# Down phase of a ConvFFN: four inner activations loaded earlier, a store moved to another queue

## The chip, the cores and the metric

The kernel runs on one core of a Trainium2 chip. The metric is the device time of one execution in microseconds. Its engines: PE (TensorE, matmuls), DVE (VectorE), ACT (ScalarE), POOL (GpSimd), and SP (SyncE), whose queue starts nearly all DMA transfers. Each engine works through its own instructions in order. Line numbers (L1347) are those of the kernel before.

## The reference, cut to what matters

Two layers work on 128 context rows and 1024 latent rows (1152 rows, 9 tiles of 128). The change lies in the ConvFFN that ends both layers:

```python
def _conv_ffn(h, w_up, conv_w, w_down):          # h: 1152 x 1024, w_up: 1024 x 5632, w_down: 2816 x 1024
    u = _dwconv(h @ w_up, conv_w)                # three taps along the rows
    a, gt = jnp.split(u, 2, axis=-1)
    return (jax.nn.silu(gt) * a) @ w_down
...
    xs = _layer_norm(ALPHA * xs + gt2_s * fs, ln2_g[l], ln2_b[l])
```

## The kernel before, in words

All matmuls are single precision made of three products of a high and a low part (`mm3`, L93 to L95): `hi` is a rounded copy made by ACT, `lo` the rest, made by DVE or POOL. For weights that is `wsplit` (L108, L109), for inner activations `split_s` (L1267, L1268).

The instructions stand in each engine's queue in the order in which the Python code issues them; no scheduler moves them. A pool gives tiles of one tag a ring of buffers; a pool that is closed gives its memory to the pools opened after it, and the first writer of new memory waits for the last readers of the tile that lay there.

**Up phase** (`ffn_up`). The 22 inner features blocks of 128 are made as pairs: block f of `a` with block f of the gate. The first three pairs are plain products, pairs p = 3 to 21 use seven products q = 0 to 6 on quarter matrices, whose weight operands are sums held in the tag `S`. The results of a pair gather in a tile `u` (two buffers, taken in turn). A pair's convolution, silu and product t1*t2 run on ACT and DVE while the next pair's products run on PE; `keep` (L1130) then stores it to DRAM as sd[l][p], from SP. The last pair (p = 21) has no next pair: its convolution runs after the last product. In its course the first two weight units of the down phase (`raws`, split into `dws`) and the activations f = 0, 1 (`sraws`, L1196) are loaded, and f = 0, 1 are split.

**Down phase** (`ffn_down`). The blocks f are taken in groups: [0, 1], then five of four. Within a group, for each half of the 1024 output columns, nine row tiles t = 8 to 0 are multiplied: 6 matmuls a tile in the first group, 12 later. A tile goes to one of six PSUM banks (`psd`). In the first group ACT copies it to y[t] (L1347), later DVE adds it (L1349). Between the tiles, weight units are split and loaded (`split_unit`, `raw_unit`) and the activations of the next group are split. `split_s` takes the oldest loaded activation and then loads the one two further into the same buffer (`sraw`, L1254). In the first group f = 2 to 5 are split behind the tiles t = 7, 5, 4, 2 of the first half. The residual stream of the groups after it uses `gb` (L298), two rows of layer-norm gains spread to all partitions, scaled on ACT behind the first tile of the second group.

SP's order at the seam: weight units 0 and 1, f = 0, 1, the store of pair 20, the store of pair 21, weight units 2 and 3, f = 2, 3, `gb`, then what the splits release.

Of the kernel before, what the change touches and what calls it, by code (L numbers as in the profile page):

```python
# [9 lines left out]
F32 = mybir.dt.float32  # L10
# [10 lines left out]
P = 128  # L21
D = 1024
KT = 8
NT = 9
# [14 lines left out]
HW = 580  # L39
HO = HW - 2  # L40
# [6 lines left out]
FGROUPS = [[0, 1], [2, 3, 4, 5], [6, 7, 8, 9], [10, 11, 12, 13], [14, 15, 16, 17], [18, 19, 20, 21]]  # L47
# [33 lines left out]
def build(tc, ins, outs, consts):  # L81
    nc = tc.nc
# [20 lines left out]
    def wsplit(raw, a, b, ring=None, eng=None):  # L103
        n = a * b
        pool, bufs = ring or (wp, 3)
        hi = pool.tile([P, 1024], F32R, tag="whi", bufs=bufs, name="whi")
        lo = pool.tile([P, 1024], F32R, tag="wlo", bufs=bufs, name="wlo")
        nc.scalar.activation(hi[:, :n], raw[:, :n], AF.Copy)  # L108
        (eng or nc.gpsimd).tensor_tensor(lo[:, :n], raw[:, :n], r32(hi[:, :n]), op=ALU.subtract)  # L109
        return (hi[:, :n].rearrange("p (a b) -> p a b", b=b),  # L110
                lo[:, :n].rearrange("p (a b) -> p a b", b=b))
# [535 lines left out]
    with ExitStack() as st:  # L647
# [185 lines left out]
        with tc.manual_schedule(engines={ET.PE, ET.Activation}):  # L833
# [3 lines left out]
            for i in range(-LEAD - 3, total + PVL):  # L837
                p = i + LEAD
# [143 lines left out]
    sraws = []  # L982
    def ffn_up(l, hT, mod_list, steps, y):
# [9 lines left out]
        ws = {0: wpre.pop(0), 1: wpre.pop(0)}  # L993
        raws = {2: wraw(*up_cols(l, 2))}
        pss, cvs = {}, {}

        def bank():
            return pd.tile([P, 512], F32, tag="d", name="psl")
# [38 lines left out]
        tp, ts, held = None, {}, None  # L1037
# [89 lines left out]
                                               op1=ALU.add)  # L1127

        def keep(p, t):
            nc.sync.dma_start(sd[l][p][:, :2 * HO].rearrange("p (a b) -> p a b", b=HO), t)  # L1130

        for n in range(N0):
            if n == 0:
# [47 lines left out]
        for p in range(P0, NP):  # L1181
            last = p == NP - 1
            u = tp.tile([P, 4, HW], F32, tag="u", bufs=2, name="u")
            us = [u[:, 2 * x:2 * x + 2, :] for x in range(2)]
            e1 = fp.tile([P, HW], F32, tag="e1", name="e1")
            for q in range(7):
                o = 7 * (p - P0) + q
                operand(o + 4)
                if last and q == 2:
                    for x in range(2):  # L1190
                        raws[x] = wraw(*down_unit(l, x))
                if last and q == 2:
                    for f in range(2):
                        raw = tp.tile([P, 4, HW], F32, tag=f"T2{f}", name="sraw").rearrange(
                            "p a b -> p (a b)")[:, :2 * HO]
                        nc.sync.dma_start(raw, sd[l][f][:, :2 * HO])  # L1196
                        sraws.append(raw)
                if last and q == 4:
                    dws[0] = wsplit(*raws.pop(0))
                if last and q > 4:  # L1200
                    split_s(l, q - 5, None)
                ps = pq.tile([P, 2, 512], F32, tag="q", name="psq")

                if old and q == 0:
                    old["t2"] = conv_first(p - 1, 1, old["us"][1])
                    conv_rest(p - 1, 1, old["us"][1], old["t2"])
                    old["t1"] = conv_first(p - 1, 0, old["us"][0])
                if old and q == 1:
                    nc.scalar.activation(old["t2"], old["t2"], AF.Silu)
                    conv_rest(p - 1, 0, old["us"][0], old["t1"])  # L1210
                if old and q == 2:
                    nc.vector.tensor_tensor(old["t1"], old["t1"], old["t2"], op=ALU.mult)
                if old and q == 3:
                    keep(p - 1, old["t1"])
                    if p == P0 + 12:
                        gate_store(l, 5)
                product(o, ps)
                add = nc.vector.tensor_tensor
                b, e = ps[:, :, :HW // 2], two(e1)
                c11, c12, c21, c22 = (two(u[:, x, :]) for x in range(4))  # L1220
                if q == 0:
                    nc.scalar.activation(e, b, AF.Copy)
                elif q == 1:
                    add(c12, e, b, op=ALU.add)
                elif q == 2:
                    add(c21, c12, b, op=ALU.add)
                elif q == 3:
                    add(c22, c21, b, op=ALU.add)
                    add(c12, c12, b, op=ALU.add)
                elif q == 4:  # L1230
                    add(c11, e, b, op=ALU.add)
                elif q == 5:
                    add(c21, c21, b, op=ALU.add)
                elif q == 6:
                    add(c12, c12, b, op=ALU.add)
                if o % 4 == 1 and p < NP - 1:
                    next(mod, None)
            old = {"us": us}
# [5 lines left out]
        conv_rest(NP - 1, 0, us[0], t1)  # L1244
        dws[1] = wsplit(*raws.pop(1))
        nc.vector.tensor_tensor(t1, t1, t2, op=ALU.mult)
        keep(NP - 1, t1)
        tps.close()
        fs.close()
# [2 lines left out]
    def sraw(l, f, pool):  # L1252
        raw = pool.tile([P, 2 * HO], F32, tag="sraw", bufs=2, name="sraw")
        nc.sync.dma_start(raw, sd[l][f][:, :2 * HO])  # L1254
        return raw
# [16 lines left out]
    def ffn_down(l, xsrc, mod_list, dw, tail, pre):  # L1272
        with ExitStack() as st:
# [31 lines left out]
            def x1_pair(n):  # L1305

                if n < 18:
                    xx = x1_tile()
                    for a in range(2):
                        hf, t = (n + a) // 9, NT - 1 - (n + a) % 9  # L1310
                        xxs[n + a] = xx[:, a * 512:(a + 1) * 512]
                        nc.sync.dma_start(xxs[n + a], rows_of(xsum, t)[:, hf * 512:(hf + 1) * 512])
            nf = 2
            raw_unit(2)
            raw_unit(3)
            while len(sraws) < 2:
                sraws.append(sraw(l, 2 + len(sraws), dw))

            gb = affine_rows(lp, l, 0)
            xsum = xh[1]  # L1320

            def residual_of(t, gb):
# [7 lines left out]
                yield  # L1330
                nc.sync.dma_start(rows_of(xsum, t), x)
                yield
            stream = [s for t in range(NT - 1, -1, -1) for s in (residual_of(t, gb),) * 6]
            mod = mod_steps(mod_list, lp, lbank, 1, 3)
            for gi, grp in enumerate(FGROUPS[:-1]):
                for hf in range(2):
                    cols = slice(hf * 512, (hf + 1) * 512)
                    units = [hf] if gi == 0 else [4 * gi - 2 + 2 * hf, 4 * gi - 1 + 2 * hf]
                    nxt = [2, 3] if units == [1] else [] if gi == 0 else [units[0] + 2, units[0] + 3]
                    last = gi == len(FGROUPS) - 2  # L1340
                    if last and hf:
                        nxt += [units[0] + 4]
                    for t in range(NT - 1, -1, -1):
                        ps = pd.tile([P, 512], F32, tag="d", name="psd")
                        products(ps, gi, t, units)
                        if gi == 0:
                            nc.scalar.activation(y[t][:, cols], ps, AF.Copy)  # L1347
                        else:
                            nc.vector.tensor_tensor(y[t][:, cols], y[t][:, cols], ps, op=ALU.add)  # L1349
                        if t in (8, 6, 3) and nxt:  # L1350
                            u = nxt.pop(0)
                            split_unit(u)
                            raw_unit(u + 2)
                        if t in (7, 5, 4, 2) and nf < FGROUPS[gi + 1][-1] + 1 and (t > 3 or gi == 0):
                            if gi == 0 or nf < FGROUPS[gi + 1][0] + 2 * (hf + 1):
                                split_s(l, nf, dw)
                                nf += 1
                        if gi == 1 and t == 1 and hf == 0:
                            gate_load(l, 5, rows)
                        if gi == len(FGROUPS) - 3 and t == 1 and hf:  # L1360
                            x1_pair(0)
                        if gi == 1 and hf == 0 and t == NT - 1:
                            nc.scalar.activation(gb, gb, AF.Copy, scale=ALPHA)
                        if gi and stream:
                            next(stream.pop(0))
                        if gi:
                            next(mod, None)
                        if last and l and t == 8 and hf == 0:
                            gb = affine_rows(lp, l, 1)
                        if last:  # L1370

                            yy = y[t][:, cols]
                            n = 9 * hf + NT - 1 - t
                            if n % 2 == 0:
                                x1_pair(n + 2)
                            nc.gpsimd.tensor_tensor(yy, yy, rows[:, cond_of(t), cols], op=ALU.mult)
                            later.append((yy, xxs.pop(n)))
                            if len(later) > 2:
                                a, b = later.pop(0)
                                nc.vector.tensor_tensor(a, a, b, op=ALU.add)  # L1380
# [733 lines left out]
```

## Time and profile before

| | us |
|---|---|
| median of three runs | 3277.81 |
| lowest, highest | 3276.28, 3280.92 |
| profiled execution, its own time | 3279.65 |
| its span, first to last instruction | 3277.9 |

PE is busy 3144.1 us (96%), DVE 2248.1 (69%), POOL 1421.4 (43%), ACT 1289.4 (39%). The granted TensorE clock is 0.986 of full speed on average. The first down group lies at 1218 to 1254 us in layer 0 and at 2971 to 3007 us in layer 1. In a timeline row the two numbers are start and length in us, then engine, line, operation, out<-in, the count of merged instructions, and in brackets how long the engine had idled and for whom.

### The profile page before, as it was taken

What the parts mean: (1) busy time and instruction counts of PE and PEld (TensorE: products, weight loads), DVE (VectorE), ACT (ScalarE), POOL (GpSimd) and SP (SyncE); (2) the same over time, 40 slices, a digit from 0 to 9 for tenths busy, and PEclk for the clock granted to TensorE, in tenths of its full rate; (3) what the DMA queues carried; (4) which work ended last, traced back from release to release, by engine and by line L of the source; (5) the groups of instructions that cost most, each with busy time, mean ns of one, the idle gap of its engine ahead of it and who ended that gap; (6) DMA issues with size and microseconds to landing.
All of it is one profiled execution on the core that took longest, in us unless ns stands there. A gap on an engine that the chain in (4) does not pass through costs nothing. (4 is left out here: it accounts for less than half of the span.)

```text
span 3277.9 us, 48732 instructions
## 1 busy us (share of the span) xinstructions
PE 3144.1 (96%) x19231; PEld 2910.5 (89%) x19231; DVE 2248.1 (69%) x3117; ACT 1289.4 (39%) x2162; POOL 1421.4 (43%) x1007
## 2 busy tenths in 40 slices
PE   7989999899999998998999999999999999998997
PEld 6989888789999997877999999999779999997886
DVE  6778888548988875674466666655556888774356
ACT  4311998333333333115433334343444333334112
POOL 6821332335545534562244343333425554443565
PEclk9999999999999999999999999999999999999999
DMA  7152000322322326541222222211331323225452
GB/s 220 35 136 90 1 1 8 129 84 68 96 92 86 89 82 210 175 153 64 95 85 75 64 68 81 59 56 37 117 116 53 100 77 97 74 68 181 150 170 84
DMA packets 267476, 305.42 MB, mean 93 GB/s; under 512 B 19587, under 2 KB 200015, under 8 KB 267248
## 3 DMA queue, kind: packets, MB, share of 16 engines
q1 hardware_dynamic: 266448, 300.67, 29.0%
q8 instruction: 152, 2.49, 0.3%
q0 software_dynamic: 800, 1.63, 0.2%
q14 instruction: 76, 0.62, 0.1%
HBM read 237.84 MB, written 64.42 MB: 92 GB/s over the span
## 5 line engine op out<-in xcount | busy, mean ns | idle before, releaser
L1098 POOL TENSOR_TENSOR wlo<-S,whi 128x512 fp32r<-128x512 f32 x152 | 245.0, 1626 | 250.8 <-ACT whi L1097 249.5
L93 PE MATMUL psd<-whi,s 128*128 128x512 f32 x720 | 286.1, 397 | 18.0 <-ACT y L1347 17.0
L109 POOL TENSOR_TENSOR wlo<-wraw,whi 128x1024 fp32r<-128x1024 f32 x78 | 196.3, 2520 | 232.5 <-ACT whi L108 221.7
L94 PE MATMUL psd<-wlo,s 128*128 128x512 f32 x720 | 285.1, 396 | 0.0
L95 PE MATMUL psd<-whi,s 128*128 128x512 f32 x720 | 285.0, 396 | 0.0
L1630 POOL TENSOR_TENSOR X<-X,tot 128x384 f32<-128x384 f32 x144 | 181.0, 1257 | 228.4 <-PE pss L1624 175.6
L1126 DVE SCALAR_TENSOR_TENSOR t<-u,fcw,t 128x1156 f32<-128x1156 f32 x152 | 262.8, 1747 | 13.5 <-ACT t L1121 10.8
L95 PE MATMUL psq<-T,wlo 128*128 128x290 f32 x912 | 270.8, 297 | 0.0
L94 PE MATMUL psq<-T,whi 128*128 128x290 f32 x912 | 270.3, 296 | 0.0
L93 PE MATMUL psq<-T,whi 128*128 128x290 f32 x912 | 270.1, 296 | 0.0
L1098 POOL TENSOR_TENSOR wlo<-wraw,whi 128x512 fp32r<-128x512 f32 x114 | 182.6, 1603 | 172.3 <-ACT whi L1097 156.6
L108 ACT ACTIVATE whi<-wraw 128x1024 fp32r<-128x1024 f32 x130 | 136.7, 1054 | 289.8 <-DMA wraw<-in_ffn_w_down_dram 120.9
L1097 ACT ACTIVATE whi<-S 128x512 fp32r<-128x512 f32 x152 | 92.9, 628 | 323.1 <-DVE S L1076 247.3
L1349 DVE TENSOR_TENSOR y<-y,psd 128x512 f32<-128x512 f32 x144 | 98.0, 684 | 170.9 <-PE psd L95 170.4
L213 DVE SCALAR_TENSOR_TENSOR macc<-mraw,sil,macc 128x512 f32<-128x512 f32 x182 | 192.1, 1095 | 7.3 <-DMA mraw<-in_w_mod_dram 7.3
L93 PE MATMUL psu<-h,whi 128*128 128x388 f32 (+1 forms) x504 | 175.0, 348 | 12.7 <-DVE sc L639 7.3
L93 PEld LDWEIGHTS psd<-whi,s 128*128 128x128 f32 x720 | 136.1, 189 | 52.3 <-ACT y L1347 19.5
L1630 DVE TENSOR_TENSOR X<-X,tot 128x384 f32<-128x384 f32 x144 | 102.5, 712 | 114.1 <-PE pss L1624 76.5
L1624 PE MATMUL pss<-X,km 128*128 128x128 f32 x1008 | 153.0, 289 | 24.3 <-POOL X L1630 10.4
L94 PE MATMUL psu<-h,whi 128*128 128x388 f32 (+1 forms) x504 | 174.4, 346 | 1.9 <-POOL h L428 1.9
L93 PE MATMUL psp<-s,whi 128*128 128x384 f32 x480 | 174.8, 364 | 0.0
L95 PE MATMUL psu<-h,wlo 128*128 128x388 f32 (+1 forms) x504 | 173.2, 344 | 0.0
(438 smaller groups left out, 10046.7 us busy)
## 6 DMA issues: line engine op xcount, KB each, us to landing
wraw<-in_ffn_w_up_dram SPq DMA_DIRECT2D x88, 512.0 KB, 3.8
mraw<-in_w_mod_dram SPq DMA_DIRECT2D x104, 256.0 KB, 2.8
sraw<-sd SPq DMA_DIRECT2D x44, 578.0 KB, 4.6
wraw<-in_ffn_w_down_dram SPq DMA_DIRECT2D x44, 512.0 KB, 4.0
sd<-t SPq DMA_DIRECT2D x38, 578.0 KB, 3.1
wraw<-in_hgrn_w_in_dram SPq DMA_DIRECT2D x40, 512.0 KB, 4.0
mraw<-in_w_mod_dram SPq DMA_DIRECT2D x28, 512.0 KB, 3.9
wraw<-in_attn_w_in_dram SPq DMA_DIRECT2D x18, 512.0 KB, 4.4
```

Of the source, the lines that this page charges most:

```text
L93: mm(ps, l[0], r[0], start=start, stop=False)
L94: mm(ps, l[0], r[1], start=False, stop=False)
L95: mm(ps, l[1], r[0], start=False, stop=stop)
L108: nc.scalar.activation(hi[:, :n], raw[:, :n], AF.Copy)
L109: (eng or nc.gpsimd).tensor_tensor(lo[:, :n], raw[:, :n], r32(hi[:, :n]), op=ALU.subtract)
L213: nc.vector.scalar_tensor_tensor(acc[:, cond, :], raw, sil[:, cond, k:k + 1], acc[:, cond, :], op0=ALU.mult, op1=ALU.add)
L1097: nc.scalar.activation(hi, src, AF.Copy)
L1098: nc.gpsimd.tensor_tensor(lo, src, r32(hi), op=ALU.subtract)
L1126: nc.vector.scalar_tensor_tensor(t, u[:, :, c0:c0 + HO], taps(p + NF * x)[c0], t, op0=ALU.mult, op1=ALU.add)
L1349: nc.vector.tensor_tensor(y[t][:, cols], y[t][:, cols], ps, op=ALU.add)
L1624: mm(ps[:, q3 * P:(q3 + 1) * P], km[:, q3 * P:(q3 + 1) * P], scan_ap(X, QAB, QAF, c0, P, hh), start=True, stop=True)
L1630: eng.tensor_tensor(x, x, t4[:, :, :, 1 - half].unsqueeze(3).to_broadcast([P, 2, nb, hh]), op=ALU.mult)
```

## The change

The activations f = 2, 3 are loaded during the last pair, at its fourth product (q = 3), into the buffer of `u` that is not the last pair's; they are split right behind t1*t2 of the last pair. The down phase then starts with loads of f = 4, 5, ahead of weight units 2 and 3; they are split behind tile t = 2 of the first half and t = 7 of the second. A memset of one column at the head of `ffn_up` makes `S` the first tag of its pool, so that the pool's memory begins with S and not with `t`; the down phase's `sraw` buffers lie on that memory. The last pair's store is started by POOL. `gb` is loaded behind the first tile of the first group's second half.

```diff
@@ ffn_up
         pss, cvs = {}, {}
+        nc.gpsimd.memset(fp.tile([P, HW], F32, tag="S", bufs=4, name="b")[:, 0:1], 0.0)
...
         def keep(p, t):
-            nc.sync.dma_start(sd[l][p][:, :2 * HO].rearrange("p (a b) -> p a b", b=HO), t)
+            (nc.gpsimd if p == NP - 1 else nc.sync).dma_start(sd[l][p][:, :2 * HO].rearrange("p (a b) -> p a b", b=HO), t)
...
+                if last and q == 3:
+
+                    raw = tp.tile([P, 4, HW], F32, tag="u", bufs=2, name="sraws").rearrange("p a b -> p (a b)")
+                    for f in (2, 3):
+                        r = raw[:, (f - 2) * 2 * HW:(f - 2) * 2 * HW + 2 * HO]
+                        nc.sync.dma_start(r, sd[l][f][:, :2 * HO])
+                        sraws.append(r)
                 if last and q > 4:
                     split_s(l, q - 5, None)
...
         nc.vector.tensor_tensor(t1, t1, t2, op=ALU.mult)
+        for f in (2, 3):
+            split_s(l, f, None)
         keep(NP - 1, t1)
@@ ffn_down
-            nf = 2
+            nf = 4
+            while len(sraws) < 2:
+                sraws.append(sraw(l, nf + len(sraws), dw))
             raw_unit(2)
             raw_unit(3)
-            while len(sraws) < 2:
-                sraws.append(sraw(l, 2 + len(sraws), dw))
-
-            gb = affine_rows(lp, l, 0)
...
-            stream = [s for t in range(NT - 1, -1, -1) for s in (residual_of(t, gb),) * 6]
...
-                        if t in (7, 5, 4, 2) and nf < FGROUPS[gi + 1][-1] + 1 and (t > 3 or gi == 0):
+                        if t in ((7, 5, 4, 2) if gi else (7,) if hf else (2,)) and nf < FGROUPS[gi + 1][-1] + 1 and (t > 3 or gi == 0):
...
+                        if gi == 0 and hf and t == NT - 1:
+                            gb = affine_rows(lp, l, 0)
+                            stream = [s for t in range(NT - 1, -1, -1) for s in (residual_of(t, gb),) * 6]
```

## Rows read from the trace of the kernel before

**Rows 1.** The page's first part: busy time, share of span, instructions.

```profile
PE 3144.1 (96%) x19231; PEld 2910.5 (89%) x19231; DVE 2248.1 (69%) x3117; ACT 1289.4 (39%) x2162; POOL 1421.4 (43%) x1007
```

**Rows 2.** Waits of PE at both seams: total us, times, longest us.

```profile
PE psd L93 <- ACT y L1347: 8.5, 2, 8.0
...
PE psd L93 <- ACT y L1347: 8.6, 1, 8.6
```

**Rows 3.** Timeline of PE, first down group of layer 0 and its successor.

```profile
1217.94 0.47 PE L93 MATMUL psd<-whi,s 128*128 128x512 f32 x1 [0.94 <-DVE u L1235]
...
1228.97 0.39 PE L95 MATMUL psd<-whi,s 128*128 128x512 f32 x1
1237.33 0.79 PE L93 MATMUL psd<-whi,s 128*128 128x512 f32 x1 [7.97 <-ACT y L1347]
...
1253.81 0.39 PE L93 MATMUL psd<-whi,s 128*128 128x512 f32 x1
```

**Rows 4.** Timeline of PE, the same of layer 1.

```profile
2970.82 0.40 PE L93 MATMUL psd<-whi,s 128*128 128x512 f32 x1
...
2981.78 0.39 PE L95 MATMUL psd<-whi,s 128*128 128x512 f32 x1
2990.73 0.79 PE L93 MATMUL psd<-whi,s 128*128 128x512 f32 x1 [8.56 <-ACT y L1347]
...
2994.73 0.60 PE L93 MATMUL psd<-whi,s 128*128 128x512 f32 x1
...
3007.36 0.39 PE L93 MATMUL psd<-whi,s 128*128 128x512 f32 x1
```

**Rows 5.** Timeline of ACT at the seam of layer 0.

```profile
1208.26 2.21 ACT L1267 ACTIVATE s<-sraw 128x1156 fp32r<-128x1156 f32 x2
...
1221.69 1.04 ACT L108 ACTIVATE whi<-wraw 128x1024 fp32r<-128x1024 f32 x1
1222.64 1.06 ACT L1347 ACTIVATE y<-psd 128x512 f32<-128x512 f32 x2
1235.63 1.17 ACT L1267 ACTIVATE s<-sraw 128x1156 fp32r<-128x1156 f32 x1 [11.93 <-DMA sraw<-sd]
```

**Rows 6.** Timeline of SP's queue, same seam: start and length until the issue ended.

```profile
1205.36 21.84 SPq L1130 DMA_DIRECT2D sd<-t  x2
1227.29 1.39 SPq L100 DMA_DIRECT2D wraw<-in_ffn_w_down_dram  x2
1228.73 2.23 SPq L1254 DMA_DIRECT2D sraw<-sd  x2
```

**Rows 7.** Timeline of DVE, same seam.

```profile
1196.24 6.71 DVE L1126 SCALAR_TENSOR_TENSOR t<-u,fcw,t 128x1156 f32<-128x1156 f32 x4 [0.98 <-ACT t L1121]
...
1214.48 1.36 DVE L1268 TENSOR_TENSOR s<-sraw,s 128x1156 fp32r<-128x1156 f32 x1
...
1223.48 3.37 DVE L1246 TENSOR_TENSOR t<-t 128x1156 f32<-128x1156 f32 x1
```

**Rows 8.** Timeline of POOL: head of layer 0's up phase, and the seam.

```profile
709.85 1.70 POOL L336 TENSOR_TENSOR ra<-ht,ra 128x256 fp32r<-128x256 f32 x2 [7.63 <-ACT ra L335]
...
1201.59 2.52 POOL L1098 TENSOR_TENSOR wlo<-S,whi 128x512 fp32r<-128x512 f32 x1 [1.32 <-ACT whi L1097]
...
1222.81 2.82 POOL L109 TENSOR_TENSOR wlo<-wraw,whi 128x1024 fp32r<-128x1024 f32 x1 [11.97 <-ACT whi L108]
```

**Rows 9.** Timelines of ACT and DVE at the seam of layer 1.

```profile
2976.63 1.06 ACT L1347 ACTIVATE y<-psd 128x512 f32<-128x512 f32 x2
...
2977.46 3.37 DVE L1246 TENSOR_TENSOR t<-t 128x1156 f32<-128x1156 f32 x1
```

**Rows 10.** DMA issues: line, queue, count, KB each, median us to landing.

```profile
ctab<-const_ctab_dram POOLq DMA_DIRECT2D x1, 512.0 KB, 4.1
```

**Rows 11.** Stretches: busy us of PE, PEld, DVE, ACT, POOL; granted clock, DMA share, GB/s.

```profile
1253.90:1304.00 50.10, 50.10 (x218) 40.69 (x217) 30.48 (x30) 11.00 (x10) 23.76 (x10) 1.00 0.61 202
2990.00:2993.00 3.00, 2.27 (x5) 1.82 (x6) 2.11 (x2) 2.71 (x5) 0.00 (x0) 0.50 0.98 331
```

## The prediction

> **What bounds the kernel now.** I read the page first: TensorE is busy 96% of the span [rows 1], so time can only come from the few stretches in which it idles or runs slowly. Next the waits of PE around both seams between up phase and down phase: one wait stands out in each layer, a product of the first group (L1347's bank) waiting 8.0 and 8.6 us for a ScalarE copy [rows 2]. Third, PE's own timeline there. The first down group is 18 tiles of 6 matmuls. In layer 0 it begins at 1217.94, runs eight tiles up to 1228.97, stands still until 1237.33, and the next group begins at 1253.81: 35.87 us [rows 3]. In layer 1 the same marks are 2970.82, 2981.78, 2990.73 and 3007.36: 36.54 us [rows 4]. Undisturbed, 48 matmuls from 2970.82 to 2981.78 are 47 steps of 0.233 us, so 108 matmuls want 25.2 us. The matmuls behind the gap are slow as well: ten from 2990.73 to 2994.73 are nine steps of 0.44 us [rows 4], so the engine comes back from its rest at a granted clock of 0.50, 1.2 of its 2.4 GHz [rows 11].
>
> Then who holds PE. ScalarE copies two tiles at 1222.64 and next stands in `split_s` (L1267) until 1235.63, 11.93 us, for a DMA into `sraw` [rows 5]; with six banks, PE gets eight tiles far and stops. Why that DMA is late is SP's timeline: its in-order queue sits at the last store of `keep` until 1227.2 (1205.36 + 21.84, two stores), because the product t1*t2 on DVE ends at 1223.48 + 3.37 = 1226.85 [rows 6, 7]. Two weight loads come next (1227.29), then the loads of the third and fourth activation (f = 2, 3) at 1228.73, into memory that this store was still reading [rows 6].
>
> **The change, part by part.**
>
> *f = 2, 3 loaded during the last pair (q = 3).* They go to the half of `u` that pair 20 used; its last reader on DVE ends at 1196.24 + 6.71 = 1202.95 [rows 7]. So both issue at about 1203, ahead of the store of pair 20 (1205.36). ScalarE wants them at 1222.7, nearly 20 us later; today's load of f = 2, issued at 1228.73 behind two weight loads, was there 6.9 us later [rows 5, 6]. They share the engines with f = 0, 1. ScalarE took those at 1208.26 for 2.21 us, and DVE makes the lo of f = 1 only at 1214.48 [rows 5, 7], so they may be 4 us later for nothing. Ends of the cost: 0, and about 3 us a layer if both added transfers went ahead of the old ones. I take 0, since they are issued behind them.
>
> *Their split behind t1*t2.* ScalarE's order becomes: `dws[1]` at 1221.69 (1.04), hi of f = 2, 3 (2.21 for two), then the copies, 0.53 each [rows 5]. Tile t = 8 is copied by 1225.5; PE wants its bank for the seventh tile at 1217.94 + 6 x 1.40 = 1226.3. DVE adds two lo's of 1.36 after 1226.85, ending 1229.6. Here is an added wait: y[4], y[3], y[2] lie in the memory of these two loads, so the copy of t = 4 waits for 1229.6 and ends at 1230.2; queued behind it on ScalarE are the other copies. PE wants that bank for the eleventh tile at 1217.94 + 14.0 = 1231.9: 1.7 us to spare. In layer 1 PE starts 1.1 us earlier against the rest: hi's from 2976.63, so copy t = 8 ends near 2979.45 where PE wants 2979.2, a loss of 0.3; DVE 2977.46 + 3.37 + 2.72 = 2983.55, copy t = 4 done 2984.2 where PE wants 2985.1 [rows 4, 9]. Taken: 0 and 0.3 us; if these chains slip, PE pays one to one past 1.7 and 0.9.
>
> *f = 4, 5 and the moved S tiles.* The one-column memset makes S the first tiles of the pool, so the two `sraw` buffers of the down phase lie over S, not over `t`. S is last read by POOL at 1201.59 + 2.52 = 1204.1 [rows 8], so f = 4, 5 issue right behind the store of pair 20, near 1206, and are wanted after 1231. The memset stands in POOL's order behind the last layer-norm power, where POOL idles 7.63 us [rows 8]; its tile's former owner is DVE's, done by then. Ends: 0 to below 1 us; taken 0.
>
> *The last store on POOL.* SP loses its wait to 1227.2. POOL waits for 1226.85 instead; behind it stands only the lo of weight unit 2, not ready before 1235. The only POOL transfer of like size landed in 4.1 us [rows 10]; ends half and twice that, so it lands at 1229 to 1236. Its readers (the 22nd activation) come four groups later. Cost 0.
>
> *Weight units 2, 3 and gb behind that.* Unit 2's load goes out as soon as POOL has split unit 0, unit 3's when POOL ends unit 1 at 1222.81 + 2.82 = 1225.63 [rows 8]; SP is held there until then, and the next load (f = 6) has its buffer only after the lo of f = 4, near 1234. f = 4 and f = 5 now split one in each half, so ScalarE passes from copy to copy with at most one split between. My count of its order has the hi of unit 2 end near 1235 and of unit 3 near 1238.4; POOL (up to 2.82 each) ends at 1241.2, group 1 begins at 1243.1 and wants unit 3 at 1244.5. gb moves back to about 1238, in front of f = 7 and unit 5; its reader is ScalarE's scaling behind the first tile of group 1, some 1247. In group 1 ScalarE copies nothing for PE, so 10 us of lateness would cost nothing.
>
> **Sum.** Layer 0: 35.87 - 25.2 - 0.1 (first matmul slow as now) = 10.6. Layer 1: 36.54 - 25.2 - 0.3 = 11.0. Together 21.6 us off the profiled 3279.65 (span 3277.9), which lies 1.8 above the median of the runs, 3277.81; so 3258.0 for that execution and 3256.2 as a median. Behind the seam PE is busy throughout (50.10 of 50.10 us, clock 1.00 [rows 11]), so it hands on all it gains.
>
> **The rivals.**
>
> *A: a shorter wait in its place.* The chain hi, hi, copies or the wait of copy t = 4 on DVE slips by 2 to 5 us, or f = 4 comes late. For it: the spare is only 0.9 us in layer 1, and DVE's t1*t2 already takes 3.37 us beside a POOL operation. Against: nothing is added ahead of it on DVE. It gives back 1 to 4 us a layer: 3258 to 3264. A rule would lead here too: if moving the store saved only its issue, f = 4 would be issued near 1227.3, land near 1232, and hold ScalarE some 1 us a layer, 3258 to 3260 (0.04 of A's chance). The row shows otherwise: SP stood 21.84 us at the two stores [rows 6], and a wait is taken off, not an issue. (Beside it: the Trainium skill, "DMA: Bandwidth & Descriptors", Issuing engines are not separate DMA queues, says that starting transfers from several engines saves only the sequencer's time to start them; no row here has two queues at work together.)
>
> *B: the loads don't come early.* If f = 2, 3 waited for the reads of the last pair, which end on DVE before t1*t2 begins at 1223.48 [rows 7], they would land at 1228.5 to 1230, and the copy of t = 8 would end 5 to 6.5 us after PE wants its bank, in place of 8, with less lost to the clock: 4 to 10 us gained, 3268 to 3274; if they waited for the store's landing as now, nothing: 3277. Against: pairs alternate the two halves of `u`, and pair 20's is not the last's.
>
> *C: slower.* The rest in the middle is gone, and the clock falls in the groups behind instead. Each matmul at the lower level costs 0.44 - 0.233 = 0.21 us [rows 4], so past 105 slow matmuls the gain is used up; 200 would give 3256 + 42 = 3298. Against: a whole group of full work at 1.00 [rows 11].
>
> **How the numbers follow.** Forecast 0.68 (own range 3253 to 3259.5), A 0.17, B 0.05 partly and 0.05 with no effect, C 0.05. About 0.2% (6.6 us) is what a measurement of this kernel can tell from no change: faster 0.88 (forecast, A, part of B), same 0.07, slower 0.05. Range 3252 to 3265: forecast and A with their ends; the spread of the three runs, 3276.28 to 3280.92, is narrower.
>
> **What would show it.** Right: no PE wait on L1347 above 0.5 us in either seam; groups of 25 to 26 us; clock 1.00 throughout; `sraw` loads of f = 2 to 5 issued before 1207; copy t = 4 waiting on DVE L1268. A PE wait on L1347 in the seventh or eleventh tile is A; `ACT <- DMA sraw` of many us at the first split is B; low clock with no idle before it is C. The forecast is wrong if group 0 still takes over 28 us, or if it takes 25 and later groups lose it again.

## The result, and the profile after

The changed kernel took 3256.59 us (median of four runs, 3253.95 to 3257.91) beside 3277.88 us of the kernel before on the same chip: ratio 0.9931, 95% interval 0.9919 to 0.9943. Measured again beside the later experiments it gave 0.9935 [0.9922, 0.9947]. The forecast was 3256.2 us in a range of 3252 to 3265. The profiled execution took 3256.72 us, 22.93 less than the 3279.65 of the profiled one before.

Lines have moved: ScalarE's copy of the first group is L1355 now (before L1347), `split_s` L1277 and L1278, its load L1264, the early load of f = 2, 3 L1206, the store L1131. The waits of PE at the seams, layer 0 (us in total, times, longest), against [rows 2]:

```profile
PE psd L93 <- DVE u L1243: 0.9, 1, 0.9
```

In layer 1 there is none left. The 0.9 us at the first matmul of layer 0 stood there before too [rows 3]; the waits of 8.5 and 8.6 us for ScalarE are gone. The first down group in PE's timeline, layer 0, from its first matmul to the first of the next group:

```profile
1218.75 0.47 PE L93 MATMUL psd<-whi,s 128*128 128x512 f32 x1 [0.94 <-DVE u L1243]
...
1243.98 0.39 PE L93 MATMUL psd<-whi,s 128*128 128x512 f32 x1
```

That is 25.23 us, against 35.87 [rows 3]. Layer 1, the same marks, and between them the seventh tile's begin:

```profile
2958.82 0.40 PE L93 MATMUL psd<-whi,s 128*128 128x512 f32 x1
...
2966.98 0.39 PE L95 MATMUL psd<-whi,s 128*128 128x512 f32 x1
2967.37 0.50 PE L93 MATMUL psd<-whi,s 128*128 128x512 f32 x1
...
2984.23 0.39 PE L93 MATMUL psd<-whi,s 128*128 128x512 f32 x1
```

25.41 us, against 36.54 [rows 4]. The step from 2966.98 to 2967.37 is 0.39 us where an undisturbed one is 0.233. The two groups together are 21.77 us shorter. The stretches of both groups and of what follows them (columns as in [rows 11]):

```profile
1218.80:1244.20 25.40, 25.40 (x109) 20.51 (x110) 14.74 (x9) 18.08 (x27) 8.77 (x4) 1.00 0.40 133
1244.20:1304.00 59.80, 59.80 (x260) 48.59 (x259) 38.45 (x37) 15.78 (x15) 31.10 (x12) 1.00 0.63 209
2958.80:2984.40 25.60, 25.60 (x111) 20.41 (x110) 15.70 (x10) 18.11 (x26) 8.78 (x4) 1.00 0.35 120
2984.40:3040.00 55.60, 55.60 (x241) 45.19 (x241) 18.41 (x23) 15.24 (x14) 29.83 (x12) 1.00 0.54 182
```

PE is busy in every microsecond of all four, at a granted clock of 1.00: nothing gained in the group is lost behind it. SP's queue at the seam of layer 0, against [rows 6]:

```profile
1203.79 0.79 SPq L1206 DMA_DIRECT2D sraws<-sd  x2
1206.16 0.32 SPq L1131 DMA_DIRECT2D sd<-t  x1
1206.58 2.11 SPq L1264 DMA_DIRECT2D sraw<-sd  x2
1211.68 15.19 SPq L100 DMA_DIRECT2D wraw<-in_ffn_w_down_dram  x2
1234.37 0.34 SPq L1264 DMA_DIRECT2D sraw<-sd  x1
...
1238.33 0.41 SPq L298 DMA_DIRECT2D gb<-in_ln_g_dram  x1
```

f = 2, 3 go out at 1203.79, f = 4, 5 behind the store of pair 20. SP still stands 15.19 us, now for the memory of weight units 2 and 3, and nothing due is queued behind them. ScalarE, DVE and POOL, same seam, against [rows 5, 7, 8]:

```profile
1222.50 1.04 ACT L108 ACTIVATE whi<-wraw 128x1024 fp32r<-128x1024 f32 x1
1223.45 2.23 ACT L1277 ACTIVATE s<-sraws 128x1156 fp32r<-128x1156 f32 x2
1225.57 2.04 ACT L1355 ACTIVATE y<-psd 128x512 f32<-128x512 f32 x4
1230.32 1.58 ACT L1355 ACTIVATE y<-psd 128x512 f32<-128x512 f32 x3 [2.71 <-DVE s L1278]
1231.76 1.18 ACT L1277 ACTIVATE s<-sraw 128x1156 fp32r<-128x1156 f32 x1
```

```profile
1224.29 3.39 DVE L1254 TENSOR_TENSOR t<-t 128x1156 f32<-128x1156 f32 x1
1227.60 2.62 DVE L1278 TENSOR_TENSOR s<-sraws,s 128x1156 fp32r<-128x1156 f32 x2
```

```profile
1223.62 2.84 POOL L109 TENSOR_TENSOR wlo<-wraw,whi 128x1024 fp32r<-128x1024 f32 x1 [11.97 <-ACT whi L108]
1227.98 0.63 POOL L1131 DMA_DIRECT2D sd<-t  x1 [1.52 <-DVE t L1254]
```

ScalarE waits once, 2.71 us, for DVE's low part of f = 3: the added wait that the prediction named. It ends before PE needs the bank.

### The profile page after: what moved, and what is told of

The parts are those of the page before. It is cut to its first block, busy times and chain, and to the rows that moved or that the text cites. A ratio compares the mean times of both kernels' runs of the same rounds, so it can differ in the third digit from the quotient of the medians.

```text
span 3254.9 us, 48740 instructions
## 1 busy us (share of the span) xinstructions
PE 3136.4 (96%) x19231; PEld 2906.1 (89%) x19231; DVE 2247.9 (69%) x3117; ACT 1288.9 (40%) x2162; POOL 1422.9 (44%) x1011
## 5 line engine op out<-in xcount | busy, mean ns | idle before, releaser
L94 PEld LDWEIGHTS psq<-T,whi 128*128 128x128 f32 x912 | 172.5, 189 | 0.0
```

The lines of the kernel that those rows point to most:

```text
L94: mm(ps, l[0], r[1], start=False, stop=False)
```

## The experiments

Line numbers are each kernel's own. T is the prediction's account: TensorE stood still because f = 2, 3 could not be in memory in time, and having them loaded and split early takes the wait away; the store's queue and the memset are cover. Its main rival, Q: what made the loads late is the store's wait at the head of SP's queue, so the store's move carries the gain. A smaller dispute is how much of the old loss was idling and how much the slow matmuls behind it.

The whole of it in one table. A group's length is read from PE's timeline as above; ratios are to the kernel before on the same chip.

| kernel | us | ratio, interval | first group, layer 0 / 1 (us) |
|---|---|---|---|
| before | | 1 | 35.87 / 36.54 |
| after | 3256.59 | 0.9931 [0.9919, 0.9943] | 25.23 / 25.41 |
| after again | 3257.50 | 0.9935 [0.9922, 0.9947] | 25.23 / 25.42 |
| e1 loads only | 3258.84 | 0.9935 [0.9922, 0.9947] | 25.23 / 25.43 |
| e2 store on SP | 3257.70 | 0.9932 [0.9919, 0.9944] | 25.22 / 25.42 |
| e3 no memset | 3260.50 | 0.9942 [0.9928, 0.9955] | 25.22 / 25.78 |
| e4 store and memory | 3268.55 | 0.9964 [0.9951, 0.9976] | 29.99 / 31.34 |
| e5 gap filled | 3280.42 | 1.0008 [0.9999, 1.0017] | 35.72 / 39.08 |
| e6 longer DVE chain | 3265.15 | 0.9962 [0.9948, 0.9975] | 29.23 / 28.79 |
| e7 gb early | 3257.41 | 0.9936 [0.9924, 0.9949] | 25.23 / 25.41 |
| e8 store only | 3279.82 | 1.0002 [0.9993, 1.0011] | 35.64 / 37.39 |

The kernel before took 3280.07 us beside e1 to e4, 3278.30 beside e5 to e7, 3279.53 beside e8. The two groups explain the times of the kernels that moved by more than the measurement: e4's are 11.08 us shorter than before's and it is 11.52 us faster; e6's are 7.37 longer than those of after again and it is 7.65 slower.

**e1: the loads alone.** The kernel after, with the store back on SP and without the memset. The early loads and splits of f = 2, 3 stay, and with them the new order of the down phase and the late `gb`.

```diff
-        nc.gpsimd.memset(fp.tile([P, HW], F32, tag="S", bufs=4, name="b")[:, 0:1], 0.0)
...
-            (nc.gpsimd if p == NP - 1 else nc.sync).dma_start(sd[l][p]...
+            nc.sync.dma_start(sd[l][p]...
```

> The changed kernel with the last store back on SP and without the memset: only f = 2, 3 are loaded and split early, and the order of the down phase stays changed. Theory T (the gain is that ScalarE finds f = 2, 3 in memory when it reaches them; everything else has spare time): SP stands at the store until about 1227.6 of layer 0, f = 4 lands near 1232.6 (ScalarE wants it at 1231.8), f = 5 waits for the landing of the store, unit 2 lands near 1237 where ScalarE wants it at 1234.3. PE has its copies in time; 0 to 2 us given back a layer: 3256 to 3261 us, ACT waits for DMA of 1 to 4 us, no PE wait above 1 us. Rival Q (the gain comes from SP's queue being free of the store, or from the memory): 3267 us or more.

It kept the whole gain. In SP's queue of this run the old wait at the store is back in full, and the load of f = 4 comes after it:

```profile
1203.39 0.80 SPq L1205 DMA_DIRECT2D sraws<-sd  x2
1205.77 21.85 SPq L1130 DMA_DIRECT2D sd<-t  x2
1227.71 3.36 SPq L1263 DMA_DIRECT2D sraw<-sd  x2
```

ScalarE feels that as one wait of 1.14 us, and behind it one of 0.84 us for weight unit 2:

```profile
1232.63 1.17 ACT L1276 ACTIVATE s<-sraw 128x1156 fp32r<-128x1156 f32 x1 [1.14 <-DMA sraw<-sd]
```

PE has no wait in the group: 25.23 us. Q falls here: 21.85 us at the head of SP's queue cost nothing once f = 2, 3 are ahead of it.

**e2: the store back on SP, the memset kept.**

```diff
-            (nc.gpsimd if p == NP - 1 else nc.sync).dma_start(sd[l][p]...
+            nc.sync.dma_start(sd[l][p]...
```

> The changed kernel with the last store back on SP, the memset kept. T: f = 4, 5 issue near 1228.0 and land near 1232.6 and 1233.5; ScalarE waits about 1 us for f = 4, which PE does not see: 3256 to 3259 us. Rival Q (SP's queue): f = 4, 5 and units 2, 3 all 21 us later than in the changed kernel and most of the gain gone, 3267 us or more.

Not to be told from after: ratios 0.9932 and 0.9931, groups of equal length.

**e3: the store on POOL, no memset.**

```diff
-        nc.gpsimd.memset(fp.tile([P, HW], F32, tag="S", bufs=4, name="b")[:, 0:1], 0.0)
```

> The changed kernel without the memset (f = 4, 5 then go over the buffers of t), the store on POOL. T: f = 4 can issue when t1*t2 is done (1227.7), f = 5 only when the store from POOL has landed (about 1232.6), and SP holds units 2 and 3 behind it; unit 2 lands near 1237.5, ScalarE waits some 3 us for it, POOL ends unit 3 near 1244.8 where PE wants it at 1245.4 (layer 1 about 1 us tighter): 3256 to 3260 us. A rival by which the memory is what counts: 3265 us or more.

Its ratio is within the measurement of after, but 3260.50 us is 0.5 us above the range that was expected, and all five runs (3259.48 to 3263.17) lie above the five of e2 on the same chip (3256.98 to 3259.13). Its trace has a reason. The buffers of f = 4, 5 lie over `t` again, which the store reads, so SP stands at them, and weight unit 2 goes out behind them; ScalarE waits for that unit:

```profile
1227.77 6.30 SPq L1263 DMA_DIRECT2D sraw<-sd  x2
1234.17 0.90 SPq L100 DMA_DIRECT2D wraw<-in_ffn_w_down_dram  x2
```

```profile
1239.05 1.06 ACT L108 ACTIVATE whi<-wraw 128x1024 fp32r<-128x1024 f32 x1 [4.12 <-DMA wraw<-in_ffn_w_down_dram]
```

PE then waits 0.3 us (layer 0) and 0.6 us (layer 1) for POOL's low part of a unit at the start of the second group. With the 0.4 us that the first group of layer 1 is longer, that makes 1.2 us; the median lies 1.7 us above e1 and 2.8 us above e2. So the memset is worth 1 to 3 us, and only when the store is on POOL: e1 has neither and lost nothing that shows.

**e4: queue and memory without the early place.** The kernel before, with memset, store on POOL and late `gb`; f = 2, 3 are loaded ahead of weight units 2, 3 into the memory of S, and are split where before split them. The half of `u` is not used.

```diff
+        nc.gpsimd.memset(fp.tile([P, HW], F32, tag="S", bufs=4, name="b")[:, 0:1], 0.0)
...
-            nc.sync.dma_start(sd[l][p]...
+            (nc.gpsimd if p == NP - 1 else nc.sync).dma_start(sd[l][p]...
...
-            raw_unit(2)
-            raw_unit(3)
             while len(sraws) < 2:
                 sraws.append(sraw(l, 2 + len(sraws), dw))
+            raw_unit(2)
+            raw_unit(3)
...
```

> The kernel before with the memset, the store on POOL, f = 2, 3 loaded ahead of units 2, 3 into the memory of S, and gb late; no use of the half of u, splits of f = 2 to 5 behind t = 7, 5, 4, 2 as before. f = 2, 3 issue near 1206 and are there in time; f = 4, 5 need the same two buffers, so they issue only behind DVE's lo of f = 2, 3 (1228.3, 1229.7) and land near 1233 and 1234, while ScalarE wants them at 1227.6 and 1230. T: ScalarE stands about 5 us at f = 4, PE waits 1 to 1.5 us in layer 0 and 2 to 3 us in layer 1: 3259 to 3263 us. Rival Q (SP's queue and the memory are the whole gain): 3256 to 3258 us.

Missed: 11.5 us came off, about half, where more was expected. SP, DVE and ScalarE of layer 0, and PE's wait there, say why:

```profile
1204.24 1.74 SPq L1255 DMA_DIRECT2D sraw<-sd  x2
1209.38 15.19 SPq L100 DMA_DIRECT2D wraw<-in_ffn_w_down_dram  x2
1226.68 11.56 SPq L1255 DMA_DIRECT2D sraw<-sd  x4
```

```profile
1225.30 2.62 DVE L1269 TENSOR_TENSOR s<-sraw,s 128x1156 fp32r<-128x1156 f32 x2
```

```profile
1233.30 1.17 ACT L1268 ACTIVATE s<-sraw 128x1156 fp32r<-128x1156 f32 x1 [7.50 <-DMA sraw<-sd]
```

```profile
PE psd L93 <- ACT y L1346: 3.0, 1, 3.0
```

f = 2, 3 are there in time. But they fill the two `sraw` buffers, so f = 4 can only be loaded when DVE has made the low part of f = 2 (1225.30 + 1.3), goes out at 1226.68, and is split at 1233.30. PE waits 3.0 us and, in layer 1, 3.6 us, and the matmuls behind the wait are slow (0.43 us a step): 29.99 and 31.34 us. The expectation had the chain right and its sizes wrong: it gave the load of f = 4 some 4.7 us where it took 6.6 (1226.68 to 1233.30), so PE was to wait 1 to 3 us a layer, and it counted nothing for the slow matmuls, 1.6 us in layer 0. The half of `u` gives the change two more buffers: in the kernel after, f = 4 goes out at 1206.58. (e4 also splits f = 2, 3 later than after does; the two were not tried apart.)

**e5: the gap filled with work.** The kernel before, with 36 matmuls on a bank that nothing else uses, ahead of the tile at which PE stands still; nobody reads their results.

```diff
+                        if gi == 0 and hf == 0 and t == 0:
+                            fill = lbank()
+                            for n in range(36):
+                                mm(fill, parts[0][0].k(0, oidx(1), P), us[0][0][:, 0, :], start=n == 0, stop=n == 35)
```

> The kernel before, with 36 further matmuls of 128x512 (8.4 us at 0.233 us each) on a bank nothing else uses, issued where TensorE stands 8.5 and 8.6 us in its first down group. Their results are read by nobody. Theory T (the group lost its 10.6 and 11.1 us as 8.5 to 8.6 us of waiting and about 2 us of matmuls at 0.43 us instead of 0.233 us after it): the wait's end stays with the transfer, so nothing of the 17.1 us comes back, but the granted clock stays at 1.00 behind it and the slow matmuls go: 3 to 5 us below the kernel before, ratio about 0.9988, and no row of 0.63 us behind the fill. Rival (all of the loss is the wait; the clock costs nothing): the same as before within 1 us. Second rival (a matmul that runs beside the transfer slows it): 1 us or more above before.

T missed: no time came back. The fill did keep the clock in layer 0 (stretch behind the gap, granted clock 1.00), and then PE stood still at the next load:

```profile
1228.83 8.53 PE L1347 MATMUL psl<-whi,s 128*128 128x512 f32 x36
1243.40 0.50 PE L93 MATMUL psd<-whi,s 128*128 128x512 f32 x1 [1.88 <-ACT y L1351]
```

```profile
1243.40:1247.40 4.00, 4.00 (x17) 3.27 (x18) 2.22 (x2) 3.53 (x6) 0.00 (x0) 1.00 0.44 155
2997.30:3001.30 4.00, 4.00 (x11) 3.15 (x12) 2.23 (x2) 3.32 (x6) 0.00 (x0) 0.57 0.52 166
```

In the kernel before, at the same place, PE had waited only 0.50 us, because its slow matmuls had used up the rest, while ScalarE waited for f = 4:

```profile
1243.82 0.51 PE L93 MATMUL psd<-whi,s 128*128 128x512 f32 x1 [0.50 <-ACT y L1347]
```

```profile
1242.11 1.17 ACT L1267 ACTIVATE s<-sraw 128x1156 fp32r<-128x1156 f32 x1 [2.80 <-DMA sraw<-sd]
```

So in layer 0 the length of before's group was set by two loads one after the other, f = 2 and then f = 4, and the lower clock lay inside the second wait: 35.72 us with it taken away, 35.87 with it (one profiled execution each). ScalarE reaches the split of f = 4 24.13 us behind the start of the group in e5 and 24.17 us behind it before. In layer 1 the group came out 2.5 us longer: a wait of 1.65 us behind the fill, one of 1.82 us at f = 4, and slow matmuls (clock 0.57) behind that. Its load of f = 2 went out 11.90 us behind the start of the group, as before, but took 7.8 us to be there where it had taken 6.3; in layer 0 the two are 7.0 and 6.9. Why was not settled, so the second rival, that matmuls beside a transfer slow it, is not excluded: the kernel lies 2.1 us above before, and the interval reaches from 0.3 us below to 5.6 us above.

**e6: a longer chain on DVE.** The kernel after, with three more additions of 128x1156 on a tile no longer used (1.36 us each), ahead of the low parts of f = 2, 3.

```diff
         nc.vector.tensor_tensor(t1, t1, t2, op=ALU.mult)
+        for n in range(3):
+            nc.vector.tensor_tensor(t2, t2, t2, op=ALU.add)
         for f in (2, 3):
```

> The kernel after, with three further VectorE additions of 128x1156 on a tile that is no longer used, put ahead of the fp32r low parts of activations 2 and 3: some 1.3 us each, about 4 us more on VectorE in each down phase. Theory T (the new wait is that of ScalarE's fifth copy for VectorE's low part of activation 3, with 0.9 to 1.7 us to spare): the copy ends 4 us later, the spare is used up, and TensorE waits about 2.1 us in the first layer and 3.0 us in the second for a bank: 5 us above the kernel after (ratio to before about 0.9947 where after has 0.9931), with a wait for the copy's line in both layers. Rival (VectorE is not on that path, the memory and queue alone decide): the same as after within 1 us.

The waits came where and as large as T said, 2.18 us (2.1 expected) and 3.10 us (3.0), both for the copy's line. ScalarE of layer 0, and PE's waits over both seams:

```profile
1233.70 1.58 ACT L1357 ACTIVATE y<-psd 128x512 f32<-128x512 f32 x3 [6.89 <-DVE s L1280]
```

```profile
PE psd L93 <- ACT y L1357: 5.3, 2, 3.1
```

The time moved 7.7 us, not 5. Most of the rest is the clock, in layer 0 alone; the stretches behind the two waits:

```profile
1234.30:1238.00 3.70, 3.65 (x9) 2.87 (x10) 1.36 (x1) 3.70 (x7) 0.00 (x0) 0.54 0.00 0
2980.50:2984.00 3.50, 3.47 (x15) 2.84 (x16) 1.36 (x1) 3.50 (x7) 0.00 (x0) 1.00 0.00 0
```

Here nothing waits behind it, so the eight steps of 0.43 us behind the wait cost PE their 1.6 us. The rival, that DVE is off this path, falls: the spare of the added wait is what the prediction counted.

**e7: gb loaded early.** The kernel after, with `gb` loaded directly behind weight units 2 and 3.

```diff
+            gb = affine_rows(lp, l, 0)
...
-                            gb = affine_rows(lp, l, 0)
```

> The kernel after, but the load of the norm's rows is issued directly behind the weight units, as the kernel before has it, so it stands on SP ahead of the reload of activations 4 and later and waits for the memory it goes into. Theory T (nothing that SP holds behind it is due before the group is nearly done): the same as after within 1.5 us, no new TensorE wait over 0.5 us. Rival (this move too carries part of the gain, since a load that stands at the head of SP's queue for some us delays those behind it): 2 us or more above after, with a wait for a transfer in the first down group.

As after, 0.9936 beside 0.9935, the groups equal to a hundredth. The move of `gb` is worth nothing that shows.

**e8: the store alone.** The kernel before with the one line of the store changed.

```diff
-            nc.sync.dma_start(sd[l][p]...
+            (nc.gpsimd if p == NP - 1 else nc.sync).dma_start(sd[l][p]...
```

> The kernel before with one line changed: the last pair's store is started by GpSimd. SP no longer waits for the product t1*t2, but weight units 2 and 3, the next loads in its queue, want memory that GpSimd still splits from until 1225.63 in layer 0, and activations 2 and 3 go into memory that the store itself reads. Theory T (the gain is in where activations 2 and 3 lie and when they are loaded, not in whose queue holds the store): at most 2 us a layer off, from SP being free about 1 to 2 us sooner, 0 to 4 us in all, TensorE still waiting 7 to 9 us in both layers. Theory Q (the wait in SP's queue is what makes the loads late): 10 to 21 us off. By the skill's rule on issuing engines: nothing, within 1 us of before.

Nothing: 1.0002. SP of layer 0 passes the store of pair 20 at once and stands elsewhere:

```profile
1207.96 0.32 SPq L1130 DMA_DIRECT2D sd<-t  x1
1213.46 15.18 SPq L100 DMA_DIRECT2D wraw<-in_ffn_w_down_dram  x2
1229.48 7.42 SPq L1254 DMA_DIRECT2D sraw<-sd  x2
```

First at the memory of weight units 2, 3, then at the loads of f = 2, 3, which want the memory of t1*t2: f = 2 goes out when the product has ended on DVE, f = 3 at 1229.48 + 7.42, when the store too has read it and landed. DVE, ScalarE and PE's waits of layer 0:

```profile
1226.08 3.38 DVE L1246 TENSOR_TENSOR t<-t 128x1156 f32<-128x1156 f32 x1
```

```profile
1244.58 1.17 ACT L1267 ACTIVATE s<-sraw 128x1156 fp32r<-128x1156 f32 x1 [2.51 <-DMA sraw<-sd]
```

```profile
PE psd L93 <- ACT y L1347: 7.5, 2, 6.1
```

Against the start of the group f = 2 goes out 1.8 us sooner than before (8.95 us behind it instead of 10.79), and PE's first wait shrank by as much, to 6.1 us. A second wait of 1.4 us at f = 4, which ScalarE splits at 1244.58 (before it was 0.5 us), and eleven slow steps of 0.43 us where before had six took most of that back. In layer 1 the group even came out 0.85 us longer. The rule named in the expectation is from the Trainium skill, "DMA: Bandwidth & Descriptors", Issuing engines are not separate DMA queues: starting transfers from several engines at once saves only the sequencer's time to start them. The time agrees with it (1.0002). The reason is another here, though: 21.84 us of waiting did leave the queue, and the same loads then waited for memory.

**after again**, the kernel after unchanged, as the common base of e6 and e7.

> The kernel after, unchanged, beside the others on the same chip so that they can be set against it: 20 to 23 us below before, ratio 0.992 to 0.994, no TensorE wait over 1 us at the two seams. A rival (the first measurement was lucky): ratio above 0.995.

As expected, 20.8 us below before.

## Why the prediction was right, step by step

- **The stall is the early load's to take away.** Shown: e1, the early loads and splits with the down phase in its new order, has the whole gain; e8, the store alone, none; e4, queue and memory, half. Not run: the early loads in the old order of the down phase, and the memory of S alone.
- **Sum.** Predicted 10.6 + 11.0 = 21.6 us; the groups measure 10.64 + 11.13 = 21.77, with 0.1 in layer 0 as before. The medians differ by 21.3 us. The profiled executions differ by 22.93; the 1.2 us beyond the two groups lie outside the seams. From the end of the first group to the beginning of the second it is 1717.01 us before, 1714.84 after and 1717.16 in e7, whose groups are as short as after's, so this is scatter between executions as far as the runs show. That the median came within 0.4 us of the forecast is finer than the measurement, and in part luck.
- **0.3 us at layer 1's seventh tile.** There: one step of 0.39 and the next of 0.33 us instead of two of 0.233, with a total of 0.25 us, and the copy it waits for in ScalarE's order behind the two splits. The rest of that group runs at 0.233 us a step.
- **The wait of copy t = 4 for DVE, with spare.** There (2.71 us on ScalarE, none on PE), and e6 measured the spare: 4.1 us more on DVE gave waits of 2.2 and 3.1 us, so about 1.9 and 1.0 us were to spare, predicted 1.7 and 0.9.
- **Store, memset and `gb` at 0.** Right singly for the store and `gb` (e2, e7: within the measurement), and within 3 us for the memset (e3). The store landed in 3.8 us, the median of its two transfers in the kernel after, in the predicted bounds (the 4.1 us of [rows 10] was not the only POOL transfer of like size, as the prediction says; another of 512 KB took 4.8):

```profile
sd<-t POOLq DMA_DIRECT2D x2, 578.0 KB, 3.8
```

  Without the memset the store's move would cost these 1 to 3 us.
- **Why the loads were late.** Here the prediction's reading is only half of it. It names SP's in-order queue, 21.84 us at the store [rows 6], and mentions the memory in passing. That was a wait indeed, but taking it off alone let f = 2 go out only 1.8 us sooner, because the loads then waited for the memory, and the kernel gained nothing (e8). The sum did not use this reading; rival A did, where it says that a wait is taken off and not an issue.
- **f = 0, 1 and weight units 2, 3, taken at 0.** The added loads delayed nothing: ScalarE begins the splits of f = 0, 1 9.68 us ahead of the group in both kernels. POOL ended unit 3 at 1241.31, predicted 1241.2, in a trace in which the group starts 0.81 us later.
- **Rival A's late f = 4, "some 1 us a layer".** The wait exists in e1 (1.14 us on ScalarE), but not on PE; A had no spare for it, and there was some.
- **Rivals B and C.** The loads left at 1203.79, and the clock stayed at 1.00 behind the seam.
- **What the sum did not say.** It took the group's whole length, so it did not matter what the length was made of. The prediction's reading beside it, PE's 8 us of rest and then slow matmuls, is incomplete: e5 shows a second load behind the first, with the slow matmuls of layer 0 inside its wait. A sum of PE's waits alone, 8.5 + 8.6 = 17.1 us [rows 2], would have come out 4.7 us short of what the groups lost. And had the change brought f = 2, 3 in time and left f = 4 as it was, half of the gain would have stayed away, as in e4.

## What to carry to other kernels

Measure a stall by the whole stretch against the same stretch undisturbed, not by its longest wait: the next late transfer can stand right behind, as here, and the wait's row doesn't show it. Before moving a transfer to another queue, ask which memory the ones queued behind it need; if it's the memory that the transfer reads, only another place for them helps. And count buffers, not only the first load: two activations early in the two only buffers moved the stall to the third.

## What the hardware showed unexpectedly

- The granted clock did not follow the length of PE's rest. In e6 a rest of 2.18 us in layer 0 was followed by 0.54, one of 3.10 us in layer 1 by 1.00; in e5 one of 1.88 us by 1.00 and one of 1.82 us by 0.57. Ahead of e6's two rests PE had worked on the group without a pause and at 1.00, 13.8 us in layer 0 and 14.0 us in layer 1; in layer 0 a pause of 0.94 us stood before that, in layer 1 none. What decides was not tried.
- Slow matmuls cost what they take only where nothing else is late: 1.6 us in layer 0 of e6, but 0.15 us in layer 0 of the kernel before, by its group beside that of e5. The stretch that holds them there:

```profile
1237.30:1246.00 8.70, 8.17 (x27) 6.27 (x28) 3.62 (x3) 5.14 (x7) 0.00 (x0) 0.80 0.61 187
```

  The Trainium skill, "TensorE: Matmul & The Clock Gate", Terms, puts the penalty at about the slow time multiplied by the missing share of the clock; an estimate by that is 8.70 x 0.20 = 1.7 us for this stretch and 3.70 x 0.46 = 1.7 us for that of e6. In e6 the measurement agrees (1.6 us); in the kernel before it does not hold for the time of the group, which lost 0.15 us by them.
